# Ordering a planned attention stage: evacuation order, staged weights in halves, one recurrence chunk begun early, and a norm mean placed later

## The chip, the cores and the metric

The kernel runs on one NeuronCore of a Trainium2 chip. TensorE (PE) multiplies matrices into PSUM, VectorE (DVE) and ScalarE (ACT) read PSUM and write SBUF, GpSimd (POOL) works on SBUF, and SyncE (SP) issues most of the transfers. The metric is the device time of one execution in microseconds (us); the median of several runs is compared. One execution was taken with the hardware profiler.

## What is computed

One layer of a hybrid encoder for 1024 tokens of width 1024, in float32:

```python
h = rmsnorm(x);  z = h @ w_in            # one projection, cut into the inputs of three mixers and their gates
y_a = hgrn2(hq, hf, hi, hg)              # gated linear recurrence, 4 heads of 128x128 state
y_b = fox(fq, fk, fv, ff)                # causal attention with a forgetting bias, 8 heads of 64, RMS-normed q and k
y_c = memory(mq, mem_kv)                 # cross attention into 256 memory tokens, 4 heads of 128
merged = sum(sigmoid(gate_i) * (y_i @ w_br_i));  x = x + merged @ w_out
h2 = rmsnorm(x);  x = x + conv_glu(h2)   # width 2816, causal conv of 3 taps on the gate branch
```

## The kernel before, in words

Every large product is made of three float32r products (`mm3`, L246): both operands are split into a high part (a cast, mostly on ACT, L254) and a low part (a subtraction, mostly on DVE, L262), and high x high, high x low and low x high are added up in one PSUM bank. A chunk of a projection (`cm_chunk`, L288) is 128 output channels for all 1024 tokens: two banks, each of 8 x 3 products of 128 x 512. Eight banks are named by use: three `pp` for projections, two `lg`, two `tr`, one `po`.

The work goes through stages: gates and memory projections first, then the forgetting attention, then the recurrence, then the merge, then the feed-forward part.

**The attention stage is written by a planner.** `Plan` (L124) holds generators; each yields an engine, a cost in us and the time from which it can start. The planner takes the request that can start first (the lower rank on a tie, then the order in its list), traces its instructions and pins the order on every engine. Times are estimates in the code: `pe_us`, `act_us`, `dve_us` (L173 to L190), 0.8 us of `SLACK` before products that read fresh data, 4 us for a load. `Ring` (L110) counts the buffers of a kind. `plan.free` tells from when an engine is free, and is empty at the start: all begin at 0. The generators with their ranks (L1320):

- `pairs` (rank 3): for each pair of heads and each half of the tokens (n = 0, 1), transposes of normed keys and queries `z` into a `tr` bank (L1034). `pair_evac` (L991, rank 2) empties the bank: for the two heads in turn one scaled cast on ACT (L1000) and one subtraction on DVE (L1004); for keys, two POOL copies each (`pair_copies`).
- `rows` (rank 2): scores (L1081, L1082), then `reduced` (rank 0): bias and maximum on DVE (L1095), exponential on ACT, scaling on POOL.
- `outcomes` (rank 1): transposes of the probabilities (L1143), a cast on ACT and a subtraction on DVE (L1157), products with the values into `po` (L1167, L1168), at the end the sum into `ybd` (L1180 to L1186).
- `value_parts` (rank 2): high and low parts of the values (POOL, then DVE L1046).
- `stage_weights` (rank 5): weights for the fill, one SP load, one cast and one subtraction for each piece of 128 x 1024 (L1206, L1208); two raw buffers, four pairs of parts.
- `fill` (rank 9): projections that keep PE busy between: the second pair's keys and queries (256 wide), those of the last two pairs (`zd`), six gates, the recurrence's values (`hid`).

`zr` tells from when normed `z` can be read; (0, 1), the second half of the first pair, stands at 4.0. Its norm (L976 to L982) is traced just ahead of the plan: squares, sums, a mean (L266), a power on POOL (L267) and a multiplication on DVE (L982).

**After the plan** `hgrn_prep(0)` (L1366) makes three chunks for the recurrence's head 0: forget gate (`w_cm[4]`), query (`w_cm[0]`), output gate (`w_cm[8]`). The weights of the first are staged by the plan, the others are loaded and split by `weights` (L276). These instructions are ordered behind the plan's last PE instruction (`tc.issue_after`, an order on that instruction's engine alone); on the other engines the framework's scheduler places them.

**The feed-forward part** starts with products of block sums (`first_products`, L1754). Between them `second_norm` (L1742) sums squares with eight small products into `po`, takes the mean on DVE (L266) and the power -1/2 on POOL. `families` (L1834) then splits four sets of four blocks, B22, T3, B21, T4, on ACT and DVE. The power is spread over the partitions by PE (L454) behind the B22 product, and the loads of the second unit's weights on POOL (L1789) are ordered behind it.

Of the kernel before, what the change touches and what calls it, by code (L numbers as in the profile page):

```python
# [8 lines left out]
F32 = mybir.dt.float32  # L9
# [5 lines left out]
P = 128  # L15
T = 1024
D = 1024
KC = D // P
# [74 lines left out]
def run_all(gen):  # L93
    for _ in gen:
        pass
# [81 lines left out]
def act_us(n):  # L177
    return 0.1 + 0.00082 * n
# [6 lines left out]
def dve_us(n):  # L185
    return 0.07 + 0.00105 * n
# [11 lines left out]
def tile_block(ctx: ExitStack, tc: tile.TileContext, xT, memT, x_rows, mem_rows, vec, fbias, mats, hmask, w_first, w_cm, w_late, w_fqk, w_fv,  # L198
# [33 lines left out]
    def col(i):  # L232
        return cv[:, i:i + 1]
# [313 lines left out]
    def gate_tile():  # L547
        return home["pool"].tile([P, HB], F32, tag="gt", name="gt", bufs=5 if home["pool"] is p0 else 3)
# [442 lines left out]
    def pair_evac(p, n, what, k, ptr, t):  # L991
        kh, kl, qa = qk[p]
        sl = slice(n * HB, (n + 1) * HB)
        gc = col(C_FK) if what == 0 else fqs
        for i in range(2):
            a = slice(64 * i, 64 * i + 64)
            o = slice(64 * (1 - i), 64 * (1 - i) + 64)
            big = kh[i] if what == 0 else qa[i]
            t = yield "ACT", 0.58, t
            S.activation(big[a, sl], ptr[a, :], AF.Copy, scale=gc[a, :])  # L1000
            low = kl[i][a, sl] if what == 0 else qa[i][o, sl]
            t = t + 0.58 + LAG
            td = yield "DVE", 0.67, t
            V.scalar_tensor_tensor(out=low, in0=ptr[a, :], scalar=gc[a, :], in1=big[a, sl].bitcast(F32),  # L1004
                                   op0=ALU.mult, op1=ALU.subtract)
# [142 lines left out]
    def outcome(h, g, sb, first, k, ptr, t):  # L1148
        c = slice(first * P, HB)
        w = HB - first * P  # L1150
        kp, tp = yield from pls.get()
        ph = pf.tile([P, HB], F32R, tag="ph", name="ph", bufs=2)
        pl = pf.tile([P, HB], F32R, tag="pl", name="pl", bufs=2)
        t = yield "ACT", act_us(w), max(t, tp)
        cast(S, ph[:, c], ptr[:, c])
        t = yield "DVE", dve_us(w), t + act_us(w) + LAG
        V.tensor_sub(pl[:, c], ptr[:, c], ph[:, c].bitcast(F32))  # L1157
# [9 lines left out]
        PE.matmul(po[:, c], vh[h][:, sb, :], ph[:, c], start=sb == 0, stop=False)  # L1167
        PE.matmul(po[:, c], vh[h][:, sb, :], pl[:, c], start=False, stop=sb == 4 * g + 3)  # L1168
        t += 2 * pe_us(w) + PE_LAG
        turn[h, g] = sb + 1  # L1170
        pls.free(kp, t)
        if sb < 4 * g + 3:
            return
        if g:
            vhs.free(h, t)
        p, i = divmod(h, 2)
        ky, ty = yield from gts.get()
        yp = gate_tile()[:64, :]
        t = yield "ACT", 0.55, max(t, ty)
        S.copy(yp, po[64:128, :])  # L1180
# [12 lines left out]
    def stage_weights(jobs):  # L1193
        for j, (src, shape, count) in enumerate(jobs):
            parts[j] = []
            for q in range(count):
                n = shape[0] * shape[1]
                kr, t = yield from raws.get()
                raw = wp.tile([P, 4 * 264], F32, tag="raw", name="raw", bufs=2)
                t = yield "SP", 0.1, t  # L1200
                SP.dma_start(raw[:, :n], src[q] if count > 1 else src)
                t += LOAD
                kw, tw = yield from ws.get()
                h, l = (wp.tile([P, 4 * 264], F32R, tag=g, name=g, bufs=WIDE) for g in ("wh", "wl"))
                t = yield "ACT", act_us(n), max(t, tw)
                cast(S, h[:, :n], raw[:, :n])  # L1206
                t = yield "DVE", dve_us(n), t + act_us(n) + LAG
                V.tensor_sub(l[:, :n], raw[:, :n], h[:, :n].bitcast(F32))  # L1208
                t += dve_us(n) + LAG
                raws.free(kr, t)  # L1210
                parts[j].append(([x[:, :n].rearrange("p (a b) -> p a b", a=shape[0]) for x in (h, l)], kw, t))

# [46 lines left out]
    def gate_evac(i, n, ps, k, t):  # L1259
# [9 lines left out]
        SP.dma_start(gd[i, n], gt)  # L1269
        gts.free(kg, t + STORE)  # L1270

    def fill(gates):
        yield from tokens(-1, 4, 256, pair_block)
        for j in range(2 + len(gates)):
            if j == 0 or j > len(gates):
                yield from tokens(j, 2, HB, to_dram(zd, zd_ready) if j == 0 else to_dram(hid, hid_ready))
                continue
            for n in range(2):
                k, t = yield from pp.get()
                ps = ps_proj()  # L1280
                sl = slice(n * HB, (n + 1) * HB)
                t = yield from steps(j, KC, HB, lambda q, h, l: mm3(ps, h[:, q, :], l[:, q, :], uh[q][:, sl], ul[q][:, sl],
                                                                   q == 0, q == KC - 1), t, n == 1)
                plan.add(1, gate_evac(gates[j - 1], n, ps, k, t))

    def later_pairs():
        for p in (2, 3):
# [26 lines left out]

    gates = list(islice(early, NFOX))
    sources = [(w_late[0], (2, HB), 4)] + [(w_cm[16 + 8 * order[i][0] + order[i][1]], (KC, P), 1) for i in gates]
    sources += [(w_late[1], (2, HB), 4), (w_cm[4], (KC, P), 1)]
    zr.update({(0, 0): 0.0, (0, 1): 4.0})
    plan = Plan(tc)
    for rank, gen in ((2, rows()), (1, outcomes()), (3, pairs()), (2, value_parts()), (2, decays()), (5, stage_weights(sources)),  # L1320
                      (4, later_pairs()), (9, fill(gates)), (6, values_back())):
        plan.add(rank, gen)
# [43 lines left out]
    def hgrn_prep(h, parts=None):  # L1366
        ph = state["ph"]
        qt = ph.tile([P, T], F32, tag="hq", name=f"hq_{h}", bufs=2)
        at = ph.tile([P, T], F32, tag="ha", name=f"ha_{h}", bufs=2)
        for what, base, dst in ((0, 4, at), (1, 0, qt), (2, 8, None)):  # L1370
            if what == 2:
                dst = gz = ph.tile([P, T], F32, tag="hz", name=f"hz_{h}", bufs=2)

            for n, ps in cm_chunk(w_cm[base + h], KC, uh, ul, h == 3 and what == 2, None if what else parts):
                sl = slice(n * HB, (n + 1) * HB)

                zt = ph.tile([P, HB], F32, tag="zt", name="zt") if h else gate_tile()
                V.tensor_mul(zt, ps, rx[:, sl])
                d = dst[:, sl]
                S.activation(d, zt, AF.Tanh, scale=0.5)  # L1380
                if what == 0:

                    G.tensor_scalar(d, d, TMIN, c1[:, h:h + 1], ALU.max, ALU.mult)
                else:

                    V.scalar_tensor_tensor(out=d, in0=d, scalar=1.0, in1=zt, op0=ALU.add, op1=ALU.mult)
                yield
        hset[h] = (qt, at, gz)
# [174 lines left out]
    open_hgrn()  # L1563
    pya = Rounded(tc, name="pya", bufs=1, side="left", reuse_waits="tile")
    ya = pya.tile([P, 4, T], F32, tag="y16", name="ya")
    with tc.issue_after(plan.last[str(PE.engine)]):
        run_all(hgrn_prep(0, parts[len(sources) - 1][0][0]))
    for h in range(3):
        weave((ahead(hgrn_mix(h, ya), AHEAD), HGRN_STEPS), (hgrn_prep(h + 1), 6))

# [171 lines left out]
    def second_norm():  # L1742
        ps = ps_po()
        for tb in range(8):
            PE.matmul(ps[:, tb:tb + 1], acc[:, tb * P:(tb + 1) * P], ones[:, 0:1], start=True, stop=True)
        late["pow"] = rstd_small(rt2, ps[:, :8], D)


    def snap(ps):
# [84 lines left out]
    def families():  # L1834

        for name, q, after in (("B22", 3, None), ("T3", 1, "e5"), ("B21", 2, "snap"), ("T4", 0, "snap")):
            with ExitStack() as order:
# [9 lines left out]
                for k in range(4):  # L1847
                    late["last"] = family_block(name, k, quarters(k)[q])
                    late["cast"] = late["split cast"]
            if name == "T3":  # L1850
                with tc.issue_after(late["cast"].ins):
                    late["e2"] = snap(late.pop("x"))
# [308 lines left out]
```

## Time and profile before

| what | us |
|---|---|
| median of 3 runs | 1711.74 (1708.91 to 1713.87) |
| the profiled execution | 1705.88 |
| its span, first to last instruction | 1704.1 |
| PE busy in the span | 1685.8 |
| DVE, ACT, POOL busy | 1163.0, 801.9, 323.9 |

The times of the trace are counted from the span's start. The attention plan lies between about 353 and 654 us, the recurrence behind it, and the feed-forward part begins at about 1066 us. In a row of the timeline stand start, duration, engine, line, operation, tiles and shape, and in brackets the idle time of that engine ahead of it and what ended it. PE's durations overlap, since matmuls are pipelined; the distance of two starts is what one costs.

### The profile page before, as it was taken

The numbers are of one execution on the slowest core, as the hardware profiler recorded it, in microseconds if no ns is written. First come the engines' busy times: TensorE is split into PE (matmuls) and PEld (weight loads), VectorE is DVE, ScalarE is ACT, GpSimd is POOL, SyncE is SP. The second block draws the span as 40 slices with busy tenths as digits, with TensorE's granted clock in tenths as the row PEclk, the third lists the DMA queues.
The fourth block names the chain that finished last, engine by engine and source line by source line (L and its number), as shares of the span: only waits on it lengthen the run. The fifth ranks groups of instructions, "written<-read, shape, count | busy, mean of one in ns | idle before, by whom it ended". The sixth has DMA issues, their size and how long they took to land.

```text
span 1704.1 us, 23210 instructions
## 1 busy us (share of the span) xinstructions
PE 1685.8 (99%) x8421; PEld 1422.6 (83%) x8421; DVE 1163.0 (68%) x2091; ACT 801.9 (47%) x1436; POOL 323.9 (19%) x428
## 2 busy tenths in 40 slices
PE   9999999989999999999999999999999999999998
PEld 7888889988877887888888888888888888888887
DVE  6966545557787655766856845887778888765654
ACT  6734335646665545655631333644434444533432
POOL 0200003254554332433301000211111111100000
PEclk9999999999999999999999999999999999999999
DMA  9442232131242222100237551566445444494772
GB/s 373 167 147 105 107 126 105 44 109 50 93 141 75 90 70 101 56 32 19 92 106 241 173 186 62 183 173 174 149 144 142 118 145 146 166 355 157 253 265 87
DMA packets 87347, 235.49 MB, mean 138 GB/s; under 512 B 9904, under 2 KB 12600, under 8 KB 87104
## 3 DMA queue, kind: packets, MB, share of 16 engines
q1 hardware_dynamic: 68320, 167.88, 27.9%
q0 software_dynamic: 18336, 65.54, 13.4%
q8 instruction: 66, 1.08, 0.3%
q10 hardware_dynamic: 576, 0.59, 0.1%
q14 instruction: 49, 0.40, 0.1%
HBM read 184.91 MB, written 72.13 MB: 151 GB/s over the span
## 4 chain that ended last, share of the span: by engine, by line
PE 95%; DVE 3%; ACT 1%; issue 1%; DMA 0%; POOL 0%; ACTq 0%; POOLq 0%
PE pp L248 20%; PE pp L250 20%; PE pp L249 20%; PE lg L248 5%; PE lg L250 5%; PE lg L249 5%; PE tr L249 3%; PE tr L248 3%; PE tr L250 3%; PE tr L1143 2%; PE po L1168 1%; PE po L248 1%; PE po L250 1%; PE po L249 1%; PE lg L1082 1%; PE lg L1081 1%
## 5 line engine op out<-in xcount | busy, mean ns | idle before, releaser
L248 PE MATMUL pp<-uh,wh 128*128 128x512 f32 x356 | 142.3, 400 | 0.0
L250 PE MATMUL pp<-uh,wl 128*128 128x512 f32 x356 | 140.5, 395 | 0.0
L249 PE MATMUL pp<-ul,wh 128*128 128x512 f32 x356 | 140.5, 395 | 0.0
L254 ACT CAST wh<-s 128x512 fp32r<-128x512 f32 x118 | 71.0, 620 | 130.8 <-PE pp L249 72.2
L248 PE MATMUL pp<-wh,uh 128*128 128x256 f32 (+2 forms) x384 | 126.2, 329 | 0.0
L249 PE MATMUL pp<-wl,uh 128*128 128x256 f32 (+2 forms) x384 | 124.1, 323 | 0.0
L250 PE MATMUL pp<-wh,ul 128*128 128x256 f32 (+2 forms) x384 | 123.8, 322 | 0.0
L254 ACT CAST wh<-rw 128x512 fp32r<-128x512 f32 x93 | 56.8, 619 | 112.5 <-PE pp L249 65.9
L254 ACT CAST wh<-raw 128x1024 fp32r<-128x1024 f32 (+2 forms) x72 | 63.4, 883 | 95.5 <-PE pp L249 84.2
L254 ACT CAST dwh<-wr 128x1024 fp32r<-128x1024 f32 (+1 forms) x41 | 40.2, 980 | 117.5 <-PE tr L249 39.4
L250 PEld LDWEIGHTS pp<-uh,wl 128*128 128x128 f32 x356 | 67.0, 188 | 13.8
L250 PEld LDWEIGHTS pp<-wh,ul 128*128 128x128 f32 x384 | 73.3, 191 | 5.7
L248 PEld LDWEIGHTS pp<-uh,wh 128*128 128x128 f32 x356 | 67.0, 188 | 12.3
L249 PEld LDWEIGHTS pp<-ul,wh 128*128 128x128 f32 x356 | 67.1, 188 | 12.2
L248 PEld LDWEIGHTS pp<-wh,uh 128*128 128x128 f32 x384 | 73.5, 191 | 4.0
L249 PEld LDWEIGHTS pp<-wl,uh 128*128 128x128 f32 x384 | 73.6, 192 | 3.9
L1157 DVE TENSOR_TENSOR pl<-tr,ph 128x512 fp32r<-128x512 f32 (+1 forms) x96 | 50.6, 551 | 31.4 <-ACT ph L254 31.1
L1116 ACT ACTIVATE pt<-pt,st 128x128 f32<-128x128 f32 (+3 forms) x64 | 49.7, 776 | 43.4 <-DVE st L1112 30.6
L262 DVE TENSOR_TENSOR dwl<-wr,dwh 128x1024 fp32r<-128x1024 f32 (+1 forms) x41 | 46.3, 1130 | 34.5 <-ACT dwh L254 33.9
L1120 POOL TENSOR_SCALAR pt<-pt,st 128x128 f32<-128x128 f32 (+3 forms) x64 | 51.6, 808 | 65.6 <-DVE st L1118 55.7
L1679 DVE TENSOR_TENSOR wl<-rw,wh 128x512 fp32r<-128x512 f32 x69 | 46.6, 687 | 21.2 <-PE pp L250 17.9
L254 ACT CAST ph<-tr 128x512 fp32r<-128x512 f32 (+1 forms) x96 | 42.9, 477 | 37.5 <-PE tr L1143 35.2
(505 smaller groups left out, 5159.6 us busy)
## 6 DMA issues: line engine op xcount, KB each, us to landing
rw<-in_w_up POOLq DMA_DIRECT2D x42, 512.0 KB, 4.9
sd<-in_w_dn POOLq DMA_DIRECT2D x30, 512.0 KB, 6.1
br<-yd SPq DMA_DIRECT2D x30, 512.0 KB, 4.9
gd<-gt SPq DMA_DIRECT2D x48, 256.0 KB, 2.1
gt<-gd SPq DMA_DIRECT2D x48, 256.0 KB, 2.7
yd<-fc SPq DMA_DIRECT2D x44, 256.0 KB, 2.1
raw<-in_w_cm SPq DMA_DIRECT2D x20, 512.0 KB, 3.3
wr<-sd SPq DMA_DIRECT2D x20, 512.0 KB, 4.3
```

The source lines that it names most:

```text
L248: PE.matmul(ps, lh, rh, start=first, stop=False, skip_group_check=more)
L249: PE.matmul(ps, lh, rl, start=False, stop=False, skip_group_check=more)
L250: return PE.matmul(ps, ll, rh, start=False, stop=last, skip_group_check=more)
L254: return S.copy(out, in_)
L262: return (sub or V).tensor_sub(l, src, h.bitcast(F32))
L1081: PE.matmul(ps[:, :w], qa[:, tsl], kh[:, s0:s0 + w], start=True, stop=False)
L1082: PE.matmul(ps[:, :w], qa[:, tsl], kl[:, s0:s0 + w], start=False, stop=True)
L1116: S.activation(pt, pt, AF.Exp, bias=st[:, 2:3], accum_out=st[:, 3:4])
L1120: G.tensor_scalar(pt, pt, st[:, 3:4], 0.0, ALU.mult, ALU.add)
L1143: PE.transpose(ptr[:, j * P:(j + 1) * P], pts[j][:, sb * P:(sb + 1) * P], ident)
L1157: V.tensor_sub(pl[:, c], ptr[:, c], ph[:, c].bitcast(F32))
L1679: late["split"] = V.tensor_sub(l, src, h.bitcast(F32))
```

## The change

Five things are edited.

1. `pair_evac` asks for both casts on ACT first and then for both subtractions on DVE, instead of in turn.
2. The planner starts with estimates of how long the engines are still busy: DVE to 7.0, ACT to 1.5, POOL to 5.5, and z's second half (with its norm) is ready at 7.0 instead of 4.0.
3. `stage_weights` casts and subtracts each piece in two halves, in turn.
4. The recurrence's first chunk, both halves, becomes the last job of the fill. `begun_evac` multiplies its two banks into gate tiles on DVE once the last head's sum has its tile. The weights of head 0's other two chunks are staged by the plan too, and `hgrn_prep(0)` takes all this up; it is ordered behind the plan's last instruction on every engine.
5. The norm's mean and power are traced behind the low parts of the B22 blocks (on DVE and on POOL, by `issue_after` the last of them) instead of right behind the small products.

```diff
         gc = col(C_FK) if what == 0 else fqs
+        bigs = [kh, qa][what]
+        ts = []
+        for i in range(2):
+            a = slice(64 * i, 64 * i + 64)
+            t = yield "ACT", 0.58, t
+            S.activation(bigs[i][a, sl], ptr[a, :], AF.Copy, scale=gc[a, :])
+            ts.append(t + 0.58 + LAG)
         for i in range(2):
             a = slice(64 * i, 64 * i + 64)
             o = slice(64 * (1 - i), 64 * (1 - i) + 64)
-            big = kh[i] if what == 0 else qa[i]
-            t = yield "ACT", 0.58, t
-            S.activation(big[a, sl], ptr[a, :], AF.Copy, scale=gc[a, :])
+            big, t = bigs[i], ts[i]
             low = kl[i][a, sl] if what == 0 else qa[i][o, sl]
-            t = t + 0.58 + LAG
             td = yield "DVE", 0.67, t
...
+        if (h, g) == (7, 1):
+            rows_done["out"] = 0.0
...
-                t = yield "ACT", act_us(n), max(t, tw)
-                cast(S, h[:, :n], raw[:, :n])
-                t = yield "DVE", dve_us(n), t + act_us(n) + LAG
-                V.tensor_sub(l[:, :n], raw[:, :n], h[:, :n].bitcast(F32))
-                t += dve_us(n) + LAG
+                t = max(t, tw)
+                for c in (slice(0, n // 2), slice(n // 2, n)):
+                    t = yield "ACT", act_us(n // 2), t
+                    cast(S, h[:, c], raw[:, c])
+                    t = yield "DVE", dve_us(n // 2), t + act_us(n // 2) + LAG
+                    V.tensor_sub(l[:, c], raw[:, c], h[:, c].bitcast(F32))
+                    t += dve_us(n // 2) + LAG
...
+    begun_rows = {}
+
+    def begun_evac(n, ps, k, t):
+        yield lambda: rows_done.get("out")
+        _, tg = yield from gts.get()
+        begun_rows[n] = gate_tile()
+        t = yield "DVE", dve_us(HB), max(t, tg)
+        V.tensor_mul(begun_rows[n], ps, rx[:, n * HB:(n + 1) * HB])
+        pp.free(k, t + dve_us(HB) + LAG)
...
-        for j in range(2 + len(gates)):
-            if j == 0 or j > len(gates):
+        for j in range(3 + len(gates)):
+            if j in (0, len(gates) + 1):
...
-                plan.add(1, gate_evac(gates[j - 1], n, ps, k, t))
+                plan.add(1, gate_evac(gates[j - 1], n, ps, k, t) if j <= len(gates) else begun_evac(n, ps, k, t))
...
-    sources += [(w_late[1], (2, HB), 4), (w_cm[4], (KC, P), 1)]
-    zr.update({(0, 0): 0.0, (0, 1): 4.0})
+    sources += [(w_late[1], (2, HB), 4), *((w_cm[i], (KC, P), 1) for i in (4, 0, 8))]
+    zr.update({(0, 0): 0.0, (0, 1): 7.0})
     plan = Plan(tc)
+    plan.free.update(DVE=7.0, ACT=1.5, POOL=5.5)
...
+            begun = parts and what == 0
+            for n, ps in begun_rows.items() if begun else cm_chunk(w_cm[base + h], KC, uh, ul, h == 3 and what == 2, parts and parts[[4, 0, 8].index(base)]):
...
-                zt = ph.tile([P, HB], F32, tag="zt", name="zt") if h else gate_tile()
-                V.tensor_mul(zt, ps, rx[:, sl])
+                if begun:
+                    zt = ps
+                else:
+                    zt = ph.tile([P, HB], F32, tag="zt", name="zt") if h else gate_tile()
+                    V.tensor_mul(zt, ps, rx[:, sl])
...
-    with tc.issue_after(plan.last[str(PE.engine)]):
-        run_all(hgrn_prep(0, parts[len(sources) - 1][0][0]))
+    with ExitStack() as behind_plan:
+        for ins in plan.last.values():
+            behind_plan.enter_context(tc.issue_after(ins))
+        run_all(hgrn_prep(0, [parts[len(sources) - 3 + i][0][0] for i in range(3)]))
...
-        late["pow"] = rstd_small(rt2, ps[:, :8], D)
+        late["norm sums"] = ps
...
+            if name == "B22":
+                with tc.issue_after(late["last"].ins):
+                    late["pow"] = rstd_small(rt2, late["norm sums"][:, :8], D)
```

More of the change, by code (lines that the diff above doesn't have):

```diff
@@ L1372, in hgrn_prep @@
                 dst = gz = ph.tile([P, T], F32, tag="hz", name=f"hz_{h}", bufs=2)
-            for n, ps in cm_chunk(w_cm[base + h], KC, uh, ul, h == 3 and what == 2, None if what else parts):
+            begun = parts and what == 0
+            for n, ps in begun_rows.items() if begun else cm_chunk(w_cm[base + h], KC, uh, ul, h == 3 and what == 2, parts and parts[[4, 0, 8].index(base)]):
                 sl = slice(n * HB, (n + 1) * HB)
-                zt = ph.tile([P, HB], F32, tag="zt", name="zt") if h else gate_tile()
-                V.tensor_mul(zt, ps, rx[:, sl])
+                if begun:
[3 more added lines that the diff above has]
+                    V.tensor_mul(zt, ps, rx[:, sl])
                 d = dst[:, sl]
```

## The prediction

> **What bounds the kernel now.** The page's busy times come first.
>
> ```profile
> PE 1685.8 (99%) x8421; PEld 1422.6 (83%) x8421; DVE 1163.0 (68%) x2091; ACT 801.9 (47%) x1436; POOL 323.9 (19%) x428
> ```
>
> PE is busy in 1685.8 us, 99% of the span, and the change takes no product away. So all that can be won are PE's idle time, some 18 us, and time at a lowered clock. The second view, PE's waits in the plan (353 to 655 us), says where half of it lies:
>
> ```profile
> PE tr L1034 <- DVE kl L1004: 5.2, 1, 5.2
> PE po L1168 <- DVE pl L1157: 2.4, 4, 0.9
> PE tr L1143 <- DVE qa L1004: 1.2, 2, 0.7
> PE po L1167 <- ACT ph L254: 0.9, 1, 0.9
> ```
>
> The reader sees one wait of 5.2 us and several near 1 us (total, count, longest). The third view cuts the plan into windows; after the window and its length follow the busy time and count of PE, PE's weight loads, DVE, ACT and POOL, then the granted clock:
>
> ```profile
> 353.00:372.00 19.00, 13.75 (x102) 13.50 (x101) 13.01 (x16) 9.21 (x15) 11.38 (x12) 0.82 0.59 198
> 372.00:480.00 108.00, 107.92 (x618) 93.26 (x617) 80.30 (x262) 67.09 (x137) 53.38 (x73) 1.00 0.27 87
> 480.00:571.00 91.00, 88.15 (x462) 72.84 (x460) 73.01 (x218) 51.32 (x104) 44.48 (x58) 1.00 0.23 76
> 640.00:654.00 14.00, 12.21 (x64) 9.84 (x63) 7.05 (x10) 8.45 (x13) 0.00 (x0) 1.00 0.38 134
> 364.00:368.00 4.00, 4.00 (x20) 3.93 (x20) 3.36 (x4) 3.57 (x6) 1.65 (x2) 0.52 0.18 45
> 368.00:370.00 2.00, 2.00 (x19) 2.00 (x18) 1.90 (x4) 1.37 (x2) 1.36 (x3) 1.00 0.88 322
> 1120.00:1160.00 40.00, 40.00 (x178) 33.16 (x177) 31.32 (x47) 16.22 (x25) 6.34 (x10) 1.00 0.62 182
> ```
>
> Idle: 5.25 us at the plan's start, 0.08 and 2.85 in its middle, 1.79 at its end. Behind the long wait the clock is about half: 20 products in 4 us where 38 are usual, 18 short at 0.105 us (2.00 / 19), **1.9 us** more.
>
> **The start of the plan (edits 1 and 2).** The timeline of all engines there:
>
> ```profile
> 354.39 0.36 PE L248 MATMUL pp<-wh,uh 128*128 128x256 f32 x1
> 354.88 2.90 POOL L267 TENSOR_TENSOR fr<-fr,mhalf 128x16 f32<-128x16 f32 x1 [10.44 <-DVE fr L266]
> 357.81 1.63 DVE L982 TENSOR_TENSOR z<-z,fr 128x1024 f32<-128x1024 f32 x1 [3.02 <-POOL fr L267]
> 358.31 0.28 PE L250 MATMUL pp<-wh,ul 128*128 128x256 f32 x1
> 359.36 2.11 DVE L1046 TENSOR_TENSOR vhl<-Vf,vhl 128x512 fp32r<-128x512 f32 x2
> 361.39 0.73 DVE L1004 SCALAR_TENSOR_TENSOR kl<-tr,cv,kh 64x512 fp32r<-64x512 f32 x1
> 362.16 0.68 ACT L1000 ACTIVATE kh<-tr,cv 64x512 fp32r<-64x512 f32 x1 [6.67 <-DVE kl L1004]
> 362.94 0.76 DVE L1004 SCALAR_TENSOR_TENSOR kl<-tr,cv,kh 64x512 fp32r<-64x512 f32 x1
> 363.64 0.47 ACT L1237 ACTIVATE z<-pp,rt 128x256 f32<-128x256 f32 x1
> 363.84 1.94 PE L1034 MATMUL tr<-ident,z 128*128 128x128 f32 x8 [5.25 <-DVE kl L1004]
> 371.96 0.22 PE L1081 MATMUL lg<-kh,qa 128*128 128x128 f32 x1
> ```
>
> DVE waits for POOL's power until 357.81, multiplies, makes two value parts, and only then empties the first `tr` bank, at 363.70. The old plan had DVE free at 0, so it put the second half's transposes on PE after some 33 fill products (354.39 to 358.31 at 0.12 us each), too early. The new order, by the code's own costs: DVE from 7.0, two value parts (2 x 0.75), two subtractions (2 x 0.67), a lag of 0.12: the bank is free at 9.96, the transposes come at 10.76. The first half's end at 1.90. So (10.76 - 1.90) / 0.342 = 26 fill steps of three products, 78 in place of 33: 9.4 us, up to about 363.8. The bank is really free at about 363.0: 359.44, two value parts of 1.05, two subtractions of 0.77, now in a row. Cover 0.75 us. The fill lasts: nothing is taken from another queue, and its evacuations on ACT (that of 363.64 stood behind the cast that waited until 362.16) come free. So the idle 5.25 and the 1.9 go: **7.15 us**. Value taken: all; the bounds are 0 (the gap only moves, below) and 7.15.
>
> Edit 1 is meant for that ACT wait. In the whole plan ACT stood idle ahead of L1000 until DVE's subtraction in 12 cases:
>
> ```profile
>   DVE kl L1004: 12.5, 7
>   DVE qa L1004: 6.2, 5
> ```
>
> That is ACT's time, not PE's. Now the first subtraction waits for the second cast, 0.6 us later, and the second for no cast at all; at the start DVE is late anyway, so nothing. The Trainium skill ("PSUM — Partial Sum Buffer", PSUM bank collisions) says that two engines may read one bank at once if they are in different groups of 32 partitions, as these two heads' halves are; by that the old wait is the program's own and the chip needs neither order. Here the trace shows the 18.7 us of waits all the same; by the page's rule alone edit 1 would be worth 0 and cost 0.6 us a bank, and no run here shows the two reads side by side.
>
> **The plan's middle.** Its 2.93 us of idle are misfits between planned and real times. The order of 280 us is drawn anew, and every one can go or double: bounds +2.9 and -2.9 of gain. I take 0, since nothing says which way.
>
> **The end (edits 3 and 4).** The fill ends 0.86 us ahead of the first row for PE below, and the last head's products stand bare:
>
> ```profile
> 650.28 1.05 ACT L254 CAST wh<-raw 128x1024 fp32r<-128x1024 f32 x1 [2.30 <-DMA raw<-in_w_cm]
> 651.36 1.23 DVE L262 TENSOR_TENSOR wl<-raw,wh 128x1024 fp32r<-128x1024 f32 x1 [2.12 <-ACT wh L254]
> 651.65 0.39 PE L1167 MATMUL po<-ph,vhl 128*128 128x256 f32 x1 [0.86 <-ACT ph L254]
> 652.97 0.38 PE L1168 MATMUL po<-pl,vhl 128*128 128x256 f32 x1 [0.93 <-DVE pl L1157]
> ```
>
> ACT and DVE split the recurrence's weights just ahead of what PE waits for. Edit 4 puts 48 products of 0.225 us (40.00 us / 178) = 10.8 us of fill there, and orders `hgrn_prep` behind the plan on every engine: the 0.86 + 0.93 = **1.79 us** go. The chunk is moved, not added, and so are its two DVE multiplications and the weights of two chunks (cast, subtraction, one SP load each, between the plan's SP stores; they wait for raw buffers, and behind them stand stores that nobody needs for some 20 us). Two of three `pp` banks are held until the last head's sum; the next chunk has the third for 5.4 us. Cover gone, each us costs one.
>
> The 10.8 us have a second use. The first scores began at 371.96, after transposes at 363.84; in the new order the transposes come at about the same time. If the eight heads, not PE, set the plan's end, PE would arrive 7.15 us early and run dry; the chunk covers 7.15 + 1.79 = 8.94 with 1.9 to spare.
>
> Halves cost a fixed part twice. Prices of 512 columns:
>
> ```profile
> L254 ACT CAST wh<-rw 128x512 fp32r<-128x512 f32 x93 | 56.8, 619 | 112.5 <-PE pp L249 65.9
> ...
> L1679 DVE TENSOR_TENSOR wl<-rw,wh 128x512 fp32r<-128x512 f32 x69 | 46.6, 687 | 21.2 <-PE pp L250 17.9
> ```
>
> ACT 2 x 0.62 - 1.05 = 0.19, DVE 2 x 0.69 - 1.23 = 0.15, for 17 pieces 3.2 and 2.6 us. DVE is idle 28 of 108 and 18 of 91 us in the two middle windows, ACT more: hidden, 0; without that cover 5.8. In return a cast of the chain waits behind at most half a piece.
>
> **The norm (edit 5).**
>
> ```profile
> 1071.83 2.18 ACT L254 CAST B22h<-x 128x512 fp32r<-128x512 f32 x4
> 1074.43 0.17 DVE L266 TENSOR_SCALAR rt<-po 128x8 f32<-128x8 f32 x1 [3.48 <-PE po L1745]
> 1074.51 2.50 DVE L262 TENSOR_TENSOR B22l<-x,B22h 128x512 fp32r<-128x512 f32 x4
> 1074.68 2.03 POOL L267 TENSOR_TENSOR rt<-rt,mhalf 128x8 f32<-128x8 f32 x1 [150.19 <-DVE rt L266]
> 1078.42 1.83 PE L454 MATMUL pp<-ident,rt 128*128 128x128 f32 x15
> 1087.16 0.68 DVE L1679 TENSOR_TENSOR wl<-rw,wh 128x512 fp32r<-128x512 f32 x1
> 1087.90 0.50 PE L250 MATMUL pp<-B11h,wl 128*128 128x512 f32 x1 [1.49 <-DVE wl L1679]
> ```
>
> The mean holds DVE's queue for 3.48 us although the first of the four B22 casts is done near 1072.4. From 1074.51 DVE works without a break to the low part at 1087.16, which PE awaits. With the mean behind, B22's low parts run from 1072.5 to 1075.0, all after them 2 us earlier, the awaited one ends at 1085.8 (before: 1087.84), ahead of PE, which was ready at 1086.4. **1.49 us** go (bounds 0 and 1.49). The mean comes 0.5 later, and with it the power (done near 1077.2, read by PE at 1078.42) and the two POOL loads behind it, whose data ACT casts last; both are covered.
>
> **The sum.** 7.15 + 0 + 1.79 + 1.49 = 10.4 us. The profiled execution's 1705.88 (its span of 1704.1 and 1.8 around it, which nothing here touches) becomes 1695.5. The median of the runs lies 5.86 above that execution (1711.74), and even the lowest run 3; with the same gain it becomes **1701.3**.
>
> **Rivals.**
>
> *The heads set the end.* PE's extra fill makes the second pair's projection ready early, so its norm, with a power of 2.9 us on POOL and sums on DVE at a better rank, falls among the copies and subtractions for the first scores. They could come 3 to 5 us later, and all heads with them. For: DVE, 80% busy in the third window, paces the heads. Against: the heads overlap, and a delay at the start is partly made up. What goes beyond the chunk's spare 1.9 is lost: heads 7 us late give back 5, 1706.4.
>
> *The same to the other side, slower.* The heads' end decides once it lies later than the cover and the other gain, 10.8 + 1.5 = 12.3 us. From the first scores at 372 to the last products at 653 they take 281 us, 35 each. All halves on the chain (5.8) and 5 us at the start make 10.8: just short, so each head needs about 0.2 us more as well. At 2.2 us more a head, 17.6 in all, the kernel is 5.3 slower: 1717. Against: PE idles only 2.93 us in the middle, and ACT gets its 18.7 us back.
>
> *The gap only moves.* If DVE's real order puts value parts or the new norm ahead, PE waits elsewhere for as long. Then 1.79 + 1.49 stay: 1708.5. Against: 0.75 us of cover, and the norm's inputs come later than the bank is freed.
>
> **How the numbers follow.** Forecast (gain 8 to 13) 0.58; heads late, gain 5 to 8, 0.18; gap moves or heads later, within 5.1 either way, 0.13; slower 0.11. A change of 0.3%, 5.1 us, is about what a measurement of this kernel can tell from none: faster 0.76, same 0.13, slower 0.11. The range takes in the middle's +2.9 and the runs' spread below (1695) and the heads' delay above (1709).
>
> **What would show it.** Right: in the window 353 to 372 PE busy near 19 and clock 1.00; L1000 no longer idle for DVE; 48 products of the chunk ahead of the plan's last head's sum or just behind; no wait at L1167 and L1168 at the end; B22l starting near 1 us after its first cast, no wait on L1679. Wrong: first scores much later than 18 us after the first transposes, PE idle at the plan's end, or new waits in its middle above 5 us.

## The result and the profile after

The changed kernel takes 1692.92 us (median of six runs). The kernel before takes 1708.62 (median of six as well; the three behind the 1711.74 of the prediction are among them, and lie higher than the other three). That is 15.7 us gained at the medians where 10.4 were forecast, and 1692.92 lies below the range's lower end of 1695. One of the six, the execution that was profiled first, took 2615.24 us at a granted clock of 0.60 throughout and is left out of the ratio, 0.9902 [0.9884, 0.9919], which compares means; the median of the other five is 1692.59. The changed kernel was profiled again as `x1_changed_again` (1692.33 us), and all rows "after" are from there. The diff moves the lines: L1000 stays, L1004 becomes L1008, L1034 L1038, L1143 L1147, L1157 L1161, L1167 and L1168 L1171 and L1172, L1679 L1704; a variant without edit 1 keeps L1004 and the numbers behind it.

The busy times of the page and PE's waits of the whole span (total, count, longest) answer to the first two fences of the prediction:

```profile
span 1690.6 us, 23252 instructions
PE 1681.5 (99%) x8421; PEld 1419.5 (84%) x8421; DVE 1165.5 (69%) x2108; ACT 805.3 (48%) x1453; POOL 322.2 (19%) x428
```

```profile
PE lg L248 <- ACT uh L437: 1.6, 1, 1.6
PE tr L353 <- POOL dull L351: 1.0, 1, 1.0
PE po L1172 <- DVE pl L1161: 0.9, 1, 0.9
PE tr L1147 <- DVE qa L1008: 0.4, 1, 0.4
PE pp L250 <- DVE wl L1704: 0.4, 1, 0.4
```

The wait of 5.2 us is gone from the list, and of the plan's other waits one of 0.9 and one of 0.4 us are left. The windows of the changed kernel and, below, two windows of before that the prediction does not show whole (columns as in the prediction):

```profile
353.00:372.00 19.00, 19.00 (x162) 19.00 (x161) 13.58 (x20) 11.80 (x21) 11.53 (x13) 1.00 0.43 143
372.00:640.00 268.00, 267.36 (x1427) 226.55 (x1426) 194.80 (x639) 157.15 (x326) 121.19 (x165) 1.00 0.28 91
640.00:654.00 14.00, 13.04 (x68) 10.63 (x67) 8.43 (x14) 6.81 (x13) 0.00 (x0) 1.00 0.53 176
654.00:664.00 10.00, 10.00 (x45) 8.26 (x45) 4.99 (x8) 4.00 (x6) 5.51 (x4) 1.00 0.20 71
```

```profile
372.00:640.00 268.00, 265.07 (x1440) 224.81 (x1439) 191.45 (x623) 152.96 (x312) 119.63 (x165) 1.00 0.25 83
654.00:664.00 10.00, 10.00 (x46) 8.27 (x45) 2.94 (x6) 0.81 (x2) 2.70 (x2) 1.00 0.53 183
```

In the first 19 us PE does 162 products instead of 102, at full clock. In the long middle it idles 0.64 us instead of 2.93, at the end 0.96 instead of 1.79. From one profiled execution to the other, 1705.88 to 1692.33, 13.55 us went:

| term | forecast | read from the two traces |
|---|---|---|
| start: idle 5.25, lowered clock 1.9 | 7.15 | 7.15 |
| middle: idle 2.93 to 0.64 | 0 | 2.3 |
| end: idle 1.79 to 0.96 | 1.79 | 0.8 |
| norm: wait 1.49 to 0.36 | 1.49 | 1.1 |
| sum | 10.4 | 11.4 |

The page gives a check: PE's idle time falls from 18.3 us (1704.1 - 1685.8) to 9.1 (1690.6 - 1681.5), by 9.2 (the four idle terms of the table make 9.5; some 0.3 us of idle time is new elsewhere), and its busy time by 4.3. Of these 4.3 the lowered clock is 1.9. The other 2.4 may be stalls too short to be counted as idle; no view names them, and executions of one kernel differ by as much. That the medians differ by still some 2 us more has to do with before, and the last runs take it up.

### The profile page after: what moved, and what is told of

Its sections match the earlier page's. It is cut to its first block, busy times and chain, and to the rows that moved or that the text cites. A ratio compares the mean times of both kernels' runs of the same rounds, so it can differ in the third digit from the quotient of the medians.

```text
span 2613.5 us, 23252 instructions
## 1 busy us (share of the span) xinstructions
PE 2606.1 (100%) x8421; PEld 1715.6 (66%) x8421; DVE 1179.6 (45%) x2108; ACT 813.5 (31%) x1453; POOL 312.9 (12%) x428
## 4 chain that ended last, share of the span: by engine, by line
PE 99%; DMA 0%; DVE 0%; ACT 0%; ACTq 0%; issue 0%
PE pp L249 21%; PE pp L248 21%; PE pp L250 21%; PE lg L250 5%; PE lg L249 5%; PE lg L248 5%; PE tr L249 3%; PE tr L250 3%; PE tr L248 3%; PE tr L1147 2%; PE lg L1086 1%; PE lg L1085 1%; PE po L1171 1%; PE po L1172 1%; PE po L248 1%; PE po L250 1%
## 5 line engine op out<-in xcount | busy, mean ns | idle before, releaser
L248 PE MATMUL pp<-uh,wh 128*128 128x512 f32 x356 | 209.3, 588 | 0.0
L249 PE MATMUL pp<-ul,wh 128*128 128x512 f32 x356 | 205.8, 578 | 0.0
L250 PE MATMUL pp<-uh,wl 128*128 128x512 f32 x356 | 205.4, 577 | 0.0
L248 PE MATMUL pp<-wh,uh 128*128 128x256 f32 (+2 forms) x384 | 174.6, 455 | 0.0
L250 PE MATMUL pp<-wh,ul 128*128 128x256 f32 (+2 forms) x384 | 174.0, 453 | 0.0
L249 PE MATMUL pp<-wl,uh 128*128 128x256 f32 (+2 forms) x384 | 173.9, 453 | 0.0
L254 ACT CAST wh<-raw 128x512 fp32r<-128x512 f32 (+2 forms) x89 | 66.0, 748 | 202.5 <-PE pp L249 178.9
L248 PEld LDWEIGHTS pp<-uh,wh 128*128 128x128 f32 x356 | 79.3, 223 | 49.2 <-issue 28.6
L249 PEld LDWEIGHTS pp<-wl,uh 128*128 128x128 f32 x384 | 99.8, 260 | 15.9 <-issue 8.0
L248 PEld LDWEIGHTS pp<-wh,uh 128*128 128x128 f32 x384 | 99.0, 258 | 16.5 <-issue 8.1
L1161 DVE TENSOR_TENSOR pl<-tr,ph 128x512 fp32r<-128x512 f32 (+1 forms) x96 | 51.2, 553 | 96.5 <-ACT ph L254 95.7
L1704 DVE TENSOR_TENSOR wl<-rw,wh 128x512 fp32r<-128x512 f32 x69 | 46.6, 687 | 62.4 <-PE pp L250 43.0
L1099 DVE CUSTOM_DVE_ANT_0 pt<-lg,nf 128x512 f32<-128x512 f32 (+2 forms) x80 | 41.6, 527 | 68.9 <-PE lg L1086 68.7
```

Of the source, the lines that this page charges most:

```text
L248: PE.matmul(ps, lh, rh, start=first, stop=False, skip_group_check=more)
L249: PE.matmul(ps, lh, rl, start=False, stop=False, skip_group_check=more)
L250: return PE.matmul(ps, ll, rh, start=False, stop=last, skip_group_check=more)
L254: return S.copy(out, in_)
L1099: V.tensor_tensor_reduce(out=pt[:, s0 + lo:s0 + hi], in0=ps[:, lo:hi], in1=bias, op0=ALU.add, op1=ALU.max, scale=1.0, scalar=-3e38, accum_ ...
L1704: late["split"] = V.tensor_sub(l, src, h.bitcast(F32))
```

## The experiments

The theory: the start's 7.15 us reach the end only because the chunk gives PE work where the heads would otherwise set the end; the terms are those of the prediction. The first rival: the start's gain stands by itself and the chunk is worth its 1.79. The second: the halves or the order of the casts carry the gain. In the ratios each kernel stands against the runs of before made with it (medians 1708.74 for x, 1709.36 for y, 1709.34 for z). The diffs are excerpts, and `...` marks what is left out.

**x1: the changed kernel again.** No edit.

> The changed kernel once more, for an undisturbed profile. By the sum of the prediction (start 7.15, end 1.79, norm 1.49, middle 0) it is 10.4 us faster than before; the measured median was 15.7 faster, so 5.3 us must show somewhere that the sum has at nothing. Theory A: the plan's middle (2.93 us of idle before) is gone too, and small stalls below 0.25 us with it; then idle and lowered clock between 353 us and the recurrence are near 0 and the norm's wait is gone. Rival B: the gain is outside the plan, in the recurrence's 200 us or the feed-forward part; then PE's waits in the plan sum to 2 us or more and the later stages are shorter than before.

1692.51 us, 0.9908 [0.9895, 0.9922]. The timeline of the start (start, duration, engine, line, tiles; all engines):

```profile
354.38 1.39 ACT L1000 ACTIVATE kh<-tr,cv 64x512 fp32r<-64x512 f32 x2 [0.37 <-PE tr L1038]
361.54 1.52 DVE L1008 SCALAR_TENSOR_TENSOR kl<-tr,cv,kh 64x512 fp32r<-64x512 f32 x2
363.97 0.60 PE L1038 MATMUL tr<-ident,z 128*128 128x128 f32 x4
365.49 0.60 PE L1038 MATMUL tr<-ident,z 128*128 128x128 f32 x4
370.24 0.22 PE L1085 MATMUL lg<-kh,qa 128*128 128x128 f32 x1
```

Both casts now run in one piece at 354.38, both subtractions in one piece from 361.54 to 363.06. The second half's transposes come at 363.97, forecast 363.8, without a wait, and the first scores at 370.24 where they came at 371.96.

**x2: the norm alone** (edit 5 on the kernel before).

```diff
-        late["pow"] = rstd_small(rt2, ps[:, :8], D)
+        late["norm sums"] = ps
...
+            if name == "B22":
+                with tc.issue_after(late["last"].ins):
+                    late["pow"] = rstd_small(rt2, late["norm sums"][:, :8], D)
```

> Before with edit 5 alone (the mean behind B22's low parts). Theory A: the wait of 1.49 us on L1679 at the first feed-forward unit goes and nothing else changes: 1.5 us faster, ratio 0.999. Rival B: edit 5 also shortens what follows, 4 us or more, ratio 0.9975 or less.

1707.64 us, 0.9992 [0.9983, 1.0001]: 1.1 us, the size of the term, with an interval that just reaches 1. Its wait in the feed-forward part, and behind it the stretch of x1 with the same edit:

```profile
PE pp L250 <- DVE wl L1679: 0.4, 1, 0.4
```

```profile
1059.52 2.18 ACT L254 CAST B22h<-x 128x512 fp32r<-128x512 f32 x4
1060.18 2.50 DVE L262 TENSOR_TENSOR B22l<-x,B22h 128x512 fp32r<-128x512 f32 x4 [1.55 <-ACT B22h L254]
1062.60 0.15 DVE L266 TENSOR_SCALAR rt<-po 128x8 f32<-128x8 f32 x1
1062.84 1.67 POOL L267 TENSOR_TENSOR rt<-rt,mhalf 128x8 f32<-128x8 f32 x1 [149.30 <-DVE rt L266]
1063.37 0.69 DVE L1805 TENSOR_TENSOR s<-rw 128x512 f32<-128x512 f32 x1 [0.62 <-PE pp L249]
1066.12 1.95 PE L454 MATMUL pp<-ident,rt 128*128 128x128 f32 x16
1074.35 0.50 PE L250 MATMUL pp<-B11h,wl 128*128 128x512 f32 x1 [0.36 <-DVE wl L1704]
```

The low parts start 0.66 us after the first cast, the mean follows without a wait, and the power is done at 1064.51, well ahead of PE's use at 1066.12. DVE then waits 0.62 us for PE, a wait that the kernel before did not have (it worked without a break from 1074.51 to 1087.84), so 0.36 of the 1.49 us stays.

**x3: the start alone** (edits 1 and 2 on the kernel before).

```diff
...
+            S.activation(bigs[i][a, sl], ptr[a, :], AF.Copy, scale=gc[a, :])
+            ts.append(t + 0.58 + LAG)
...
-    zr.update({(0, 0): 0.0, (0, 1): 4.0})
+    zr.update({(0, 0): 0.0, (0, 1): 7.0})
     plan = Plan(tc)
+    plan.free.update(DVE=7.0, ACT=1.5, POOL=5.5)
```

> Before with edits 1 and 2 alone (casts first, planner's starting times), no chunk in the fill. The gap of 5.25 us at the plan's start and the lowered clock go (7.15). Theory A, PE sets the plan's end: 7 us faster, ratio 0.996. Rival, the eight heads set it: PE runs out of fill about 7 us earlier and waits at the plan's end; idle there of 5 us or more, 0 to 3 us faster.

1705.58 us, 0.9981 [0.9973, 0.999]: 3.2 us, less than half of 7.15. Its wait near the plan's end, and its window there below that of before:

```profile
PE tr L1147 <- POOL pt L1124: 7.2, 2, 4.6
625.00:656.00 31.00, 23.27 (x113) 18.19 (x111) 18.90 (x50) 16.49 (x29) 5.71 (x8) 0.89 0.42 125
```

```profile
625.00:656.00 31.00, 29.21 (x147) 24.09 (x146) 15.10 (x39) 15.39 (x26) 4.91 (x7) 1.00 0.36 119
```

PE is early and has nothing left to fill with: it waits 7.2 us for the last head's probabilities, idles 7.73 us of these 31 where it idled 1.79, and the clock is lowered once more. The wait has only moved from 363 to 640 us.

**x4: all without the chunk** (edits 1, 2, 3 and 5).

```diff
-        for j in range(3 + len(gates)):
-            if j in (0, len(gates) + 1):
+        for j in range(2 + len(gates)):
+            if j == 0 or j > len(gates):
...
-    with ExitStack() as behind_plan:
-        for ins in plan.last.values():
-            behind_plan.enter_context(tc.issue_after(ins))
-        run_all(hgrn_prep(0, [parts[len(sources) - 3 + i][0][0] for i in range(3)]))
+    with tc.issue_after(plan.last[str(PE.engine)]):
+        run_all(hgrn_prep(0, parts[len(sources) - 1][0][0]))
```

> The changed kernel without edit 4: the recurrence's first chunk and weights stay behind the plan. If PE sets the plan's end it loses only the plan's bare end: 1 to 3 us slower than the changed kernel. If the heads set it, it loses most of the chunk's 10.8 us: PE idle at the plan's end of 6 to 10 us and the granted clock falls below 1 there, 7 to 12 us slower than the changed kernel.

1702.16 us, 0.9963 [0.995, 0.9975]. On top of the other edits the chunk is worth 9.6 us, more than five times its 1.79. Without it PE runs dry again:

```profile
PE tr L1147 <- POOL pt L1124: 3.0, 1, 3.0
625.00:656.00 31.00, 26.67 (x112) 20.48 (x111) 16.67 (x46) 14.22 (x25) 4.92 (x7) 0.83 0.38 124
```

4.33 us idle, and in the 26.67 busy ones 112 products where before's rate (147 in 29.21) gives 134. By this estimate, which takes the products for alike, the lowered clock costs about as much as the idle time ((134 - 112) products of 0.2 us, 4.4 us).

**y4: the chunk alone** (edit 4 on the kernel before).

```diff
-        for j in range(2 + len(gates)):
-            if j == 0 or j > len(gates):
+        for j in range(3 + len(gates)):
+            if j in (0, len(gates) + 1):
...
-    sources += [(w_late[1], (2, HB), 4), (w_cm[4], (KC, P), 1)]
+    sources += [(w_late[1], (2, HB), 4), *((w_cm[i], (KC, P), 1) for i in (4, 0, 8))]
```

> Before with edit 4 alone. The gap at the plan's start stays. If the chunk only fills what the heads leave PE (the bare end, 1.8 us idle and a lowered clock there in some runs), it is 2 to 4 us faster than before (ratio 0.9975 to 0.999) and the chunk's products run behind the last head's. If the chunk were worth its 10.8 us by itself, the ratio would be 0.994.

1704.87 us, 0.9973 [0.9963, 0.9984]: 4.5 us.

```profile
625.00:656.00 31.00, 31.00 (x158) 26.01 (x157) 16.57 (x45) 16.00 (x28) 5.34 (x8) 1.00 0.36 120
```

No idle time is left at the end. Norm, start and chunk alone sum to 1.1 + 3.2 + 4.5 = 8.8 us, and together the five edits give some 16 (and the four without the halves too, y3 below). The theory holds, the first rival falls: start and chunk are worth more together than apart. But 4.5 is well above the 1.79 of the prediction; the last runs take that up. The traces cannot: the one profiled here, 1705.87 us, is the slowest of y4's eight runs, and that of before, 1705.88, its quickest trace.

**y1, y2, y3: the changed kernel with one edit taken away**, the casts first, the planner's start times, the halves.

```diff
-            S.activation(bigs[i][a, sl], ptr[a, :], AF.Copy, scale=gc[a, :])
-            ts.append(t + 0.58 + LAG)
```

```diff
-    zr.update({(0, 0): 0.0, (0, 1): 7.0})
+    zr.update({(0, 0): 0.0, (0, 1): 4.0})
     plan = Plan(tc)
-    plan.free.update(DVE=7.0, ACT=1.5, POOL=5.5)
```

```diff
-                for c in (slice(0, n // 2), slice(n // 2, n)):
-                    t = yield "ACT", act_us(n // 2), t
+                t = yield "ACT", act_us(n), max(t, tw)
+                cast(S, h[:, :n], raw[:, :n])
```

> The changed kernel without edit 1: casts and subtractions of a bank in turn again. Theory A: edit 1 matters only through ACT's blocked queue. ACT stands idle for DVE ahead of L1000's cast again, 12 us or more in the plan, the fill's evacuations stand behind it, and PE gets a wait for a pp bank at the plan's start of 1 to 4 us: 1 to 4 us slower than the changed kernel. Rival: the planner's starting times alone do it all: within 1 us of the changed kernel.

> The changed kernel without edit 2: the planner starts all engines at 0 and takes z's second half as ready at 4.0. Theory A: the transposes of the second half come too early again, PE waits 4 to 5.5 us at about 358 us and the clock falls to one half: 7 us lost there, of which the spare at the plan's end gives back about 1: 5 to 6.5 us slower than the changed kernel. Rival: the heads set the plan's end and the chunk runs behind them anyway: 0 to 2 us slower.

> The changed kernel without edit 3: staged weights as whole pieces. Theory A: the halves removed the small waits of the plan's middle (2.4 us on L1168, 1.2 us on L1143 before): 1 to 3 us slower than the changed kernel. Rival: the halves do nothing and the redrawn order did it: within 1 us.

Without the casts first 1693.39 us, 0.9911 [0.9894, 0.9927]; without the halves 1692.82, 0.9905 [0.989, 0.9919]: neither can be told from the changed kernel. In y1 ACT stands idle ahead of L1000 for DVE again, and it costs nothing:

```profile
  DVE kl L1004: 5.9, 6
  DVE qa L1004: 4.1, 6
```

In the changed kernel only PE ends ACT's idle time there (`PE tr L1038: 3.2, 3`). y2 was the surprise: 1708.15 us, 0.9997 [0.9988, 1.0006]. Without the start times not 7 us are lost but all 16. The wait at the start is back, and there is a second stretch that neither before nor the changed kernel has; its waits and its window, and that of the changed kernel below:

```profile
PE tr L1038 <- DVE kl L1008: 5.2, 1, 5.2
PE tr L1147 <- DVE kl L1008: 2.1, 1, 2.1
391.00:412.00 21.00, 15.60 (x77) 12.45 (x76) 17.97 (x52) 15.25 (x30) 15.87 (x20) 0.84 0.27 82
```

```profile
391.00:412.00 21.00, 20.49 (x107) 16.33 (x107) 14.98 (x46) 14.25 (x27) 11.82 (x20) 1.00 0.18 57
```

5.4 us idle, and a lowered clock behind them: 77 products where there are 107. SP's queue in y2 and, below, the same load in the changed kernel:

```profile
394.79 0.51 SPq L1192 DMA_DIRECT2D ybd<-gt  x1
395.40 0.52 SPq L1058 DMA_DIRECT2D nf<-negFd  x1
396.02 0.38 SPq L1207 DMA_DIRECT2D raw<-in_w_late  x1
```

```profile
355.53 18.62 SPq L1207 DMA_DIRECT2D raw<-in_w_late  x4
```

In y2 the fourth load of late weights stands on SP behind the store of head 0's result, at which SP waits for 24.0 us (22.1 in z2, below), and is issued at 396.02; in the changed kernel all four are issued between 355.53 and 374.15. The fill then lacks weights just when PE could use it. That this makes the stretch is argued from the order alone. Which edit, beside the old start times, draws that order was the next question.

**z1, z2, z3: which edits go together.** All have the chunk and the norm; z1 has the start times (both of the first and the third diff of the y runs), z2 only the halves, z3 only the casts first.

```diff
-            S.activation(bigs[i][a, sl], ptr[a, :], AF.Copy, scale=gc[a, :])
...
-                for c in (slice(0, n // 2), slice(n // 2, n)):
```

```diff
-            S.activation(bigs[i][a, sl], ptr[a, :], AF.Copy, scale=gc[a, :])
...
-    plan.free.update(DVE=7.0, ACT=1.5, POOL=5.5)
```

```diff
-                for c in (slice(0, n // 2), slice(n // 2, n)):
...
-    plan.free.update(DVE=7.0, ACT=1.5, POOL=5.5)
```

> Before with edits 2, 4 and 5 only: neither casts first nor halves. Taking either one away cost nothing measurable. Theory A: the starting times and the chunk carry the gain together; within 2 us of the changed kernel, ratio 0.991. Rival: edits 1 and 3 stand in for each other, and without both ACT's queue delays the heads: 4 us or more slower than the changed kernel, with new waits in the plan's middle.

> Before with edits 3, 4 and 5: old starting times. Without edit 2 (edits 1, 3, 4, 5) the kernel had a second stretch of waits at 396 to 411 us: the fourth load of the late projection's weights stood on SP behind head 0's store and the third head's decay, and the fill ran dry. Theory A: the halves make each piece's planned staging longer and push that load behind head 0 on SP; then this kernel has the second stretch too and lies within 2 us of before (ratio 0.999). Rival, the casts' order does it: no second stretch, 5 to 6 us faster than before (the sum of chunk 4.5 and norm 1.3), ratio 0.9965.

> Before with edits 1, 4 and 5: old starting times, whole pieces. Theory A (the halves push the load back): no second stretch of waits, 5 to 7 us faster than before, ratio 0.996 to 0.997. Rival (the casts' order does it): the second stretch at about 396 us, ratio 0.999.

z1 1696.56 us, 0.9928 [0.9914, 0.9943]; z2 1709.38, 1.0001 [0.9992, 1.001]; z3 1701.0, 0.9954 [0.9937, 0.997]. The same window of z2 and of z3:

```profile
391.00:412.00 21.00, 17.77 (x84) 14.11 (x83) 18.41 (x59) 14.24 (x30) 15.43 (x20) 0.84 0.21 69
```

```profile
391.00:412.00 21.00, 21.00 (x114) 17.80 (x113) 17.63 (x58) 15.42 (x29) 16.28 (x22) 1.00 0.25 82
```

Halves with the old start times make the second stretch, with the casts first (y2) or without (z2); whole pieces do not. In z2 the four late loads stand together on SP, but the next load of weights for the fill stands behind the same store:

```profile
396.25 0.50 SPq L1188 DMA_DIRECT2D ybd<-gt  x1
397.47 0.41 SPq L1203 DMA_DIRECT2D raw<-in_w_cm  x1
```

In z3 that load is issued at 390.54, ahead of the store at 395.92, and in the changed kernel at 381.27. So both kernels with the stretch have their next load of weights behind head 0's store, and those without have it ahead. No run moved this load alone, so the cause of the stretch is still argued.

z3 against y3 is the start times alone, on the same other edits: 1701.0 - 1692.82 = 8.2 us, where the prediction had 7.15. (z3's trace also has a wait of 1.2 us in the merge that y3's has not, `PE pp L248 <- DVE gt L1642: 1.2, 1, 1.2`.) z1 against y1 and y3 shows that casts first and halves do count together, some 3 to 4 us, though either alone can be missed; of z1's expectation the rival comes out, not theory A. PE's idle time in windows of the four kernels that have start times, chunk and norm says where:

| kernel | casts first | halves | 353 to 372 | 372 to 640 | 640 to 664 |
|---|---|---|---|---|---|
| x1 | yes | yes | 0.00 | 0.64 | 0.96 |
| y1 | no | yes | 0.88 | 0.57 | 0.00 |
| y3 | yes | no | 0.00 | 0.98 | 0.97 |
| z1 | no | no | 1.40 | 2.51 | 0.97 |

Either edit takes most of the 2.93 us out of the middle; with neither, 2.51 stay, and the second half's transposes wait for the subtractions once more (`PE tr L1034 <- DVE kl L1004: 1.4, 2, 0.8`). z1's 4.88 us of idle are 2.9 to 3.4 more than the others', and it is 3.2 to 4.1 slower. With the old start times casts first do the same: 0.99 us of idle in the middle in z3, 3.85 in y4, which has neither casts first nor the norm; z3 is 3.9 us quicker, of which the norm is 1.1 (their intervals just overlap).

**z4: what is left at the end.** In x1 the last products stand behind this on DVE:

```profile
650.60 1.22 DVE L262 TENSOR_TENSOR wl<-raw,wh 128x1024 fp32r<-128x1024 f32 x1 [1.50 <-PE po L1171]
651.75 0.61 DVE L1161 TENSOR_TENSOR pl<-tr,ph 128x256 fp32r<-128x256 f32 x2
652.22 0.39 PE L1172 MATMUL po<-pl,vhl 128*128 128x256 f32 x1 [0.94 <-DVE pl L1161]
```

This low part belongs to the recurrence's head 1, whose `hgrn_prep` edit 4 does not order behind the plan. z4 orders it there on ACT and DVE.

```diff
+    def after_plan(gen):
+        while True:
+            with ExitStack() as order:
+                for eng in (S, V):
+                    order.enter_context(tc.issue_after(plan.last[str(eng.engine)]))
+                try:
+                    next(gen)
+                except StopIteration:
+                    return
+            yield
...
-        weave((ahead(hgrn_mix(h, ya), AHEAD), HGRN_STEPS), (hgrn_prep(h + 1), 6))
+        weave((ahead(hgrn_mix(h, ya), AHEAD), HGRN_STEPS), (hgrn_prep(h + 1) if h else after_plan(hgrn_prep(1)), 6))
```

> The changed kernel, with ACT's and DVE's instructions of the recurrence's preparation of head 1 also ordered behind the plan. In the changed kernel a low part of those weights (1.22 us on DVE) still stood ahead of the last head's subtraction, and PE waited 0.9 us at its last products. Theory A: that wait shrinks to 0.5 us or less: 0.5 to 1 us faster than the changed kernel, near what a measurement can tell. Rival: the weights of head 1 come late then, and PE waits for them behind head 0's chunks: slower by 1 us or more.

1691.45 us, 0.9899 [0.9884, 0.9914], the lowest median of all, though the intervals of z4 and x1 overlap. The rows show that the wait itself is gone: the last subtraction comes first, the split behind it.

```profile
649.98 0.65 DVE L1161 TENSOR_TENSOR pl<-tr,ph 128x256 fp32r<-128x256 f32 x2 [1.74 <-ACT ph L254]
650.46 0.38 PE L1172 MATMUL po<-pl,vhl 128*128 128x256 f32 x1
653.08 2.34 DVE L262 TENSOR_TENSOR wl<-raw,wh 128x1024 fp32r<-128x1024 f32 x2
```

**w1, w2, w3: the kernel before, profiled three more times**, for the 2 us between the profiled executions' difference and the medians', and for y4's 4.5. No edit.

> Before, unchanged, profiled again. The profiled execution on which the prediction's sum rests (1705.88) lies about 3 us below the median of before's runs. Theory A: in most executions the waits at the plan's end lower the clock a second time, or one more wait stands in the merge (both showed in the kernel with the norm alone, whose plan is that of before): then this trace has a lowered clock near 655 us or a wait near 922 us and a time of 1707.5 to 1710. Rival: the executions differ evenly everywhere; then neither shows and the time is still above 1707.

> Before, unchanged, once more: by theory A an execution with one lowered stretch and no wait in the merge is near 1706, one with two of the three is at 1707.5 to 1710; by the rival the time does not go with them.

> Before, unchanged, a third time: by theory A an execution with one lowered stretch and no wait in the merge is near 1706, one with two of the three is at 1707.5 to 1710; by the rival the time does not go with them.

1710.08, 1707.25 and 1709.09 us, all above the 1705.88 on which the prediction rests. The window behind the plan's end, of w1 and of w2:

```profile
654.00:664.00 10.00, 9.73 (x37) 8.00 (x38) 3.76 (x8) 1.88 (x3) 0.54 (x1) 0.83 0.61 211
```

```profile
654.00:664.00 10.00, 10.00 (x39) 8.10 (x38) 2.51 (x6) 0.63 (x1) 2.09 (x2) 0.85 0.52 177
```

In w3 it holds 36 products at clock 0.83. Each of the three has a second lowered clock there, and so has x2, whose plan is that of before; the execution of the prediction had 46 products and clock 1.00. The waits ahead of it are the same two, a little longer. PE's timeline of w1 gives the price:

```profile
652.95 0.39 PE L1167 MATMUL po<-ph,vhl 128*128 128x256 f32 x1 [1.02 <-ACT ph L254]
654.27 0.38 PE L1168 MATMUL po<-pl,vhl 128*128 128x256 f32 x1 [0.94 <-DVE pl L1157]
...
654.67 0.74 PE L248 MATMUL pp<-uh,wh 128*128 128x512 f32 x1
...
658.14 0.40 PE L250 MATMUL pp<-uh,wl 128*128 128x512 f32 x1
```

Eight products of 512 columns start between 654.67 and 658.14, 0.43 us each, against the 0.225 of the prediction: 3.47 - 1.80 = 1.7 us. In the changed kernel and in y4 the clock there is 1.00. So the chunk takes away 1.79 + 1.7 = 3.5 us in most executions of before, which lies inside y4's interval (2.7 to 6.3 us). The expectation's other sign, a wait in the merge, stands in w1 alone of the three (`PE pp L248 <- DVE gt L1620: 1.0, 1, 1.0`) and in x2 (0.9). The signs do not make the whole time: w2 and w3 have the same ones and lie 1.84 us apart, and w2 falls 0.25 short of the 1707.5 that was expected.

## Why the prediction was wrong in size

The mechanisms at the start, at the end and in the norm were as forecast; the gain was some 5 us short, and the time fell just below the range. Of the 8.4 us between 1701.3 and 1692.92, 3.1 are the starting point: the three runs behind 1711.74 lay high, and six give 1708.62. The other 5.3 are the gain, 15.7 instead of 10.4. The chances had no branch for a gain above 13.

- **The start, 7.15: right.** PE is busy 19.00 of 19, at clock 1.00, the transposes come at 363.97, and taking the start times out of the kernel without halves costs 8.2 us (z3 against y3).
- **"The 10.8 us have a second use": right, and the most important sentence.** Without the chunk 3.2 of the 7.15 us arrive (x3); with it all of them. The heads do set the plan's end: the last head's last products start at 652.50 in x1 and at 653.25 before, only 0.75 us earlier, and the gain lies in the chunk's products, which are done by then (DVE multiplies its two banks from 652.28 on). That they could come 3 to 5 us later for the power on POOL did not happen: the first scores come 1.72 us earlier.
- **"Its 2.93 us of idle are misfits ... I take 0": the first step that failed.** 2.3 us of them went, inside the bound of 2.9; with them went 2.4 us of busy time whose nature is open. The term had a source that the prediction priced at nothing, edits 1 and 3: with either of them 0.57 to 0.98 us of idle are left in the middle, with neither 2.51 (z1). Why the two can stand in for each other is open, since each draws the order of 280 us anew.
- **"the median ... with the same gain": the second step that failed.** The one profiled execution was the quick one of five traces of before's plan; the others lose some 1.7 us more at the plan's end, by the lowered clock behind the two waits, of which the chunk leaves one. The part of the median above the profiled execution was carried over as untouched, and a part of it was a price of the very waits that the end term counted. The end was mis-sized: 1.79 idle, of which 0.83 goes in x1, and 1.7 of clock.
- **The norm, 1.49: 1.1.** What comes behind the mean is held by PE for 0.62 us.
- **Edit 1 at nothing: right by itself** (y1), and edit 3 too (y3), the two together not (z1). For edit 1 the Trainium skill ("PSUM — Partial Sum Buffer", PSUM bank collisions) speaks of reads in different groups of 32 partitions; the time agrees with a worth of 0 beside edit 3 (y1), not without it (z1, and z3 against y4), and ACT's waits for the other half's read stood in the trace of before all the same (18.7 us) and in y1 (10.0).
- **The rival on the slower side** did not come: from the first scores to the last products the heads take 282.3 us in x1 (370.24 to 652.50) and 281.3 before.

## What to carry to other kernels

A stall's gain at the start of a stage reaches its end only if PE has work left for where the other engines' chain then ends; look for that work before counting the gain, and test the two edits together, since apart they showed 8.8 of 16 us. Profile the kernel before more than once: when the median lies above the profiled execution, ask which stage loses more in the ordinary executions, because a change may remove just that. Edits to a planned order are not additive (halves with the old start times lost the whole gain), so an edit that looks free must be tried with its neighbours, and with those taken away together.

## What the runs showed of the hardware

Two waits of about 1 us each, 1.02 and 0.94 in w1 with 0.4 us of products between them, were followed by 3.5 us at half clock, in four of five traces of before's plan; in the fifth the waits were 0.86 and 0.93, and the clock stayed at 1.00. In x1 one wait of 0.94 alone left it at 1.00, and so did the one of 1.00 in w1's merge. The Trainium skill ("TensorE: Matmul & The Clock Gate", Why this matters for your kernels) warns of idle gaps above about 3 us; in these four traces two shorter ones close together were followed by a lowered clock as well. Whether the sum of the waits or their place decides was not tried.
